# Token sums in four column groups, delta-net logits from one operand, two recurrences at a time, and a changed plan

## The chip, the core and the metric

The kernel runs on one core of one Trainium2 chip. The metric is the device time of one execution in microseconds (us). Its engines are TensorE (PE in the profile, its weight loads PEld), VectorE (DVE), ScalarE (ACT), GpSimd (POOL) and SyncE (SP, which only starts DMAs here); each runs its own instructions strictly in order. All weights come from device memory (HBM).

## The reference

A trunk of two layers: a gated delta-net with a SwiGLU network, then a forgetting attention with a SwiGLU network.

```python
# T = 512 tokens, D = 1024; 8 delta-net heads of 128; 16 forgetting-attention heads of 64; D_FF = 2816
def rms_norm(x, w): return x * rsqrt(mean(x * x) + eps) * w

def gated_deltanet_mixer(h, w_in, conv_w, a_log, dt_bias, out_norm, w_out):
    q, k, v, z, b_logit, a_in = split(h @ w_in)              # b_logit, a_in: 8 + 8 columns
    q, k, v = silu(causal_depthwise_conv(q, k, v; conv_w))   # 4 taps
    q, k = l2_normalize(q) * 128 ** -0.5, l2_normalize(k)    # per token and head
    beta, g = sigmoid(b_logit), -exp(a_log) * softplus(a_in + dt_bias)
    # per head: S_t = a_t (I - b_t k_t k_t^T) S_{t-1} + b_t k_t v_t^T,  o_t = S_t^T q_t
    o = gated_delta_rule_chunked(q, k, v, g, beta)           # triangular solve in chunks, state S carried on
    return (rms_norm(o, out_norm) * silu(z)) @ w_out

for layer in range(2):
    h = rms_norm(x, pre_mix_norm[layer])
    mix = gated_deltanet_mixer(h) if layer == 0 else forgetting_attention(h, shared k, v, gates of x)
    x = x + rms_norm(mix, post_mix_norm[layer])
    f = (silu(gate) * up) @ w_ffn_out                        # gate, up = rms_norm(x) @ w_ffn_in
    x = x + rms_norm(f, post_ffn_norm[layer])
```

## The kernel before

**Layout.** Activations lie with features on the 128 partitions and the 512 tokens along the free dimension, eight tiles for D = 1024. Weights come in units of 512 KB, eight 128x128 blocks each. Values are split into a high and a low half in a 32-bit matmul format (`fp32r`): ACT rounds the high half (`wh` of a weight, the first part of a `b` or `h` pair of an activation), DVE or POOL subtracts it to get the low half (`wl`, the second part). `product` then makes three matmuls of 512 columns per block: high by high, low by high, high by low. A unit is 24 matmuls into one PSUM bank. There are three banks for these projections (`prj`), two for general use (`mid`), two small ones (`sm`) and one for outputs (`ob`).

**The start.** `main` loads the gains, eight x tiles (`a`), the first weights and the constants, splits x times gain into eight b pairs, and sums the squares of x into one tile (`w_124`) on ACT and DVE. The first unit of keys, k0, goes block by block beside `w_small`, 16 columns with the logits of beta and the decay; per block the logits take three matmuls of their own, of 16 columns. The sums of squares are reduced over features by `token_sums`: for each chunk of 128 tokens a matmul whose weights are the 128x128 squares and whose moving operand is one column of ones; it is in plain fp32, which PE runs as two passes. DVE and POOL turn the result into `tokr` and `tokn`, four PE transposes spread `tokn`, ACT copies the rows as n0.rs, and the task `gates` makes beta and the decays. The constants negb, identb and SLR are cast on DVE.

**The delta-net part.** Units follow in the order k0 to k7 (with z0 to z2 between), z3 to z7, then q0, v0, q1, v1 and so on to v7. Behind each unit a task works on: `k_post`, `q_post` (both use `token_sums` for the norms), `v_post`, `z_post`. `inverse` inverts the chunks' 32x32 triangular blocks on DVE for all heads at once; `merge` puts a pair of heads' blocks together into 128x128, by 32x32 and 64x64 matmuls (into `mid`). `recurrence(hd)` then walks four chunks in series: state times keys on PE (`sm<-S,b`), rhs on DVE, a matmul (`sm<-rhs,b`), y on ACT, a matmul to the new state (`sm<-y,w`), S on DVE; the outputs go through `ob`. At the end the output o is scaled, transposed and gated, and split into the b pair `og[hd]`. A recurrence starts when the inverse, q and v of its head are there and the recurrence of the head before is done (signal `s{hd-1}`).

**What sets the order.** Nothing is issued as it is written. A planner (`Plan`) notes each instruction with a cost, tasks are generators that are resumed when what they wait for is done by these costs, and `ordered` then groups the instructions, sorts them in four rounds of list scheduling by the same costs, and issues them; what it gives is each engine's fixed order. Tiles come from rings ("b" has 23, "w" and "a" 8), and a ring's tiles are first written in the order in which they were asked for: an output tile of a later head's convolution is not written before the og pair that was asked for ahead of it. `next_halves` decides by the planned backlog of DVE (over 4 us) whether POOL makes a unit's low half. All instructions are recorded in one line of `Item.issue`, L102 of the profile, so the tile names tell the place.

Of the kernel before, what the change touches and what calls it, by code (L numbers as in the profile page):

```python
# [17 lines left out]
P = 128  # L18
T = 512
# [101 lines left out]
class Plan:  # L121
# [80 lines left out]
    def cost(self, eng, op, out, ins, kw):  # L202

        n = 1
        for d in out.shape[1:]:
            n *= d
        psum = any("PSUM" in str(a.space) for a in ins)
        if eng == "SP" or op == "dma_start":
            return n * 4 * out.shape[0] / 380e3, 2.0
        if eng == "PE":  # L210
            w = ins[0]
            rows, cols = w.shape[0], out.shape[0]
            if w.dtype == F32R:
                t = max(0.109, n / 2400 + 0.0135)
            elif w.dtype == BF16:
                t = n / 2400 + 0.01
            elif op == "transpose":
                t = 0.109
            elif rows <= 32:
                t = 0.026  # L220
            elif rows <= 64:
                t = 0.117
            elif cols == 64:
                t = 0.112 * n / P
            else:
                t = 2 * max(0.111, n / 1200)
            self.grid = (w.dtype == F32R, rows <= 32, rows <= 64, cols <= 64)
            return t, 0.2
        if eng == "ACT":
            m = 1  # L230
            for d in ins[0].shape[1:]:
                m *= d
            t = (m + (172 if psum else 224)) / 1200
            if not isinstance(kw.get("scale", 1.0), float):
                t += 0.09
            if kw.get("accum_out") is not None:
                t += 0.19
            return t, 0.06
        if eng == "POOL":
            if op == "memset":  # L240
                return 0.1 + n / 960, 0.06
            return (0.5 + n * 0.13 if kw.get("op") == ALU.pow else 0.1 + n * 2.28e-3), 0.06
        if op == "tensor_reduce":
            n = 1
            for d in ins[0].shape[1:]:
                n *= d
        if op == "transpose":
            return n * 2.05e-3, 0.06
        fast = op in ("tensor_copy", "tensor_scalar", "memset") and not psum
        t = (n / (2 if fast else 1) + (207 if op == "scalar_tensor_tensor" else 155)) / 960  # L250
        if op == "tensor_scalar" and n > 32:
            t += 0.055
        return t, 0.06
# [179 lines left out]
def trunk(  # L433
# [221 lines left out]
    def next_halves():  # L655

        i = len(ready)
        landing()
        late = plan.free["DVE"] - plan.now()
        slow = late > 4.0 and used[0] < i  # L660
        for go in halve(dve=POOL if slow else DVE):
            go()
        landing()
        signal(f"half{i}")
# [60 lines left out]
            dve.tensor_tensor(out=acc[:, tok], in0=acc[:, tok], in1=sq[:, tok], op=ALU.add)  # L725

    def token_sums(ps, src, chunks):
        for c in chunks:
            PE.matmul(ps[:, c : c + 1], lhsT=src[:, ck(c)], rhs=ones[:, 0:1], start=True, stop=True)

    def token_rsqrt(acc, tok, r, use):

# [210 lines left out]
    def gates(ps, n0):  # L943
        yield ("n0.rs0",)
        ba = small([P, NC, 16], "ba", 1)
        yield from token_logits(ps, n0, ba, 1)
        ealog = small([P, GH], "ealog", 1)
        ACT.activation(ealog, heads_sb[:, 0:8], AF.Exp)
        ta = small([P, NC, GH], "sp", 5)
# [227 lines left out]

    def recurrence(hd):
        kT, AT, E = KA[hd // 2][0][:, hd % 2], KA[hd // 2][1][:, hd % 2], EG[hd // 2][:, hd % 2]
        yield (f"T{hd // 2}", f"q{hd}", f"v{hd}") + ((f"s{hd - 1}",) if hd else ()) + ("#mid",)  # L1180
        qT, PT = Q[hd]
        vu = V[hd]
        ps = mid()
# [3 lines left out]
        for c in range(NC - 1):  # L1187
            DVE.tensor_scalar(
                out=kd[:, ck(c)], in0=ps[:, ck(c)], scalar1=E[:, c * P + P - 1 : c * P + P], scalar2=None, op0=ALU.mult
            )  # L1190
        ms = small([P, NC], "ms", 2)
        junk = small([P, P], "junk", 1)
        o = w_tile()
        S = None
        for c in range(NC):
            rhs = vu[:, ck(c)]
            if S is not None:
                yield (plan.ready(S), "#sm", "#ob")
                ps = sm()
                PE.matmul(ps[:, :P], lhsT=kT[:, ck(c)], rhs=S, start=True, stop=True)  # L1200
                rhs = small([P, P], "rhs", 2)
                DVE.scalar_tensor_tensor(
                    out=rhs, in0=ps[:, :P], scalar=eGn[:, c, hd : hd + 1], in1=vu[:, ck(c)], op0=ALU.mult, op1=ALU.add
                )
# [3 lines left out]
            yield (plan.ready(rhs), "#sm")  # L1208
            ps = sm()
            PE.matmul(ps[:, :P], lhsT=AT[:, ck(c)], rhs=rhs, start=True, stop=True)  # L1210
            y = small([P, P], "y", 2)
            ACT.activation(y, ps[:, :P], AF.Copy, scale=w_t[:, c, hd : hd + 1])
            yield (plan.ready(y), "#sm", "#ob")
            if c < NC - 1:
                ps = sm()
                PE.matmul(ps[:, :P], lhsT=kd[:, ck(c)], rhs=y, start=True, stop=True)
                S2 = small([P, P], "S", 3)
                if S is None:
                    DVE.tensor_copy(S2, ps[:, :P])
                else:  # L1220
                    DVE.scalar_tensor_tensor(
                        out=S2, in0=S, scalar=egl[:, c, hd : hd + 1], in1=ps[:, :P], op0=ALU.mult, op1=ALU.add
                    )
# [324 lines left out]
    for kind, hd in GDN_ORDER:  # L1548
        add(w_gdn["qkvz".index(kind) * GH + hd], DVE)
        if (kind, hd) == ("k", 0):  # L1550
            add(w_small[0], DVE, cols=16)
    out_units(w_gdn_out, 0, KT, eng)

    def ffn_units(layer):
# [24 lines left out]
    def main():  # L1579
# [69 lines left out]
        for kind, hd in GDN_ORDER:  # L1649
# [7 lines left out]
            if (kind, hd) == ("k", 0):  # L1657
                yield ("#prj",)
                ws, pb = [unit(), unit()], prj()
                for k in range(KT):  # L1660
                    product(ps, ws[0], k, h[k], k == 0, k == KT - 1)
                    product(pb[:16], ws[1], k, h[k], k == 0, k == KT - 1)
                    yield (plan.ready(h[min(k + 1, KT - 1)][:, 1]),)
                spawn(gates(pb, n0), -3)
            else:
# [136 lines left out]
```

## Time and profile before

| | us |
|---|---|
| median of 3 runs | 1345.64 (1343.53 to 1346.58) |
| the profiled execution | 1346.76 |
| its span, first to last instruction | 1345.0 |
| PE busy | 1324.7 |
| DVE busy | 770.7 |
| ACT busy | 588.7 |
| POOL busy | 121.3 |

The span is what the profile's rows add up to; the execution's own time has a little around it. Busy shares are means over stages with different limits, so the parts below are read stage by stage: windows give the busy time and TensorE's granted clock (1.00 is 2.4 GHz, 0.50 is 1.2 GHz) in a stretch, the timeline gives single instructions with the idle time ahead of them and what ended it.

### The profile page before, as it was taken

The page shows a single profiled execution, that of the slowest core. Times are in us where ns is not written, and L with a number is a line of the kernel's source. Part 1 is how long each engine was busy: PE and PEld are TensorE (multiplying, and loading weights), DVE is VectorE, ACT ScalarE, POOL GpSimd, SP SyncE. Part 2 cuts the span into 40 slices and gives each one's busy share as a digit, 9 for nine tenths or more (in the row PEclk, how much of TensorE's full clock was granted, in tenths as well). Part 3 has the DMA queues.
Part 4 walks back from the last instruction along what each step waited for, and adds up shares of the span by engine and source line. Part 5 has one row for each costly group of instructions (what it writes and reads, how often), then busy time and mean ns, then how long its engine had stood idle before and what let it go on. Part 6 is the DMA issues. An engine that isn't in the chain of part 4 may idle for free.

```text
span 1345.0 us, 18447 instructions
## 1 busy us (share of the span) xinstructions
PE 1324.7 (98%) x7290; PEld 1105.5 (82%) x7290; DVE 770.7 (57%) x1352; ACT 588.7 (44%) x1111; POOL 121.3 (9%) x109
## 2 busy tenths in 40 slices
PE   8999998999999999999999999999999999999998
PEld 5788887888988888888889787777998888888886
DVE  6978876665864442234448577687675444442223
ACT  5474455555542222232236365685653322233221
POOL 1021000001410000000003321200220000000000
PEclk8999997999999999999999999999999999999999
DMA  6312220113233323332341322210423333333221
GB/s 200 97 47 95 79 64 32 48 48 122 83 110 94 95 89 98 97 107 94 96 139 34 95 82 64 63 49 1 126 79 94 94 94 99 103 97 96 77 95 63
DMA packets 36390, 115.65 MB, mean 86 GB/s; under 512 B 6304, under 2 KB 6560, under 8 KB 36304
## 3 DMA queue, kind: packets, MB, share of 16 engines
q1 hardware_dynamic: 34432, 111.95, 26.5%
q10 hardware_dynamic: 1872, 2.53, 0.6%
q8 instruction: 57, 0.93, 0.3%
q14 instruction: 29, 0.24, 0.1%
HBM read 112.30 MB, written 2.16 MB: 85 GB/s over the span
## 4 chain that ended last, share of the span: by engine, by line
PE 96%; DVE 1%; ACT 1%; DMA 1%; issue 1%; POOL 0%; DVEq 0%; POOLq 0%; ACTq 0%
PE prj L102 76%; PE mid L102 8%; PE sm L102 7%; PE ob L102 6%; DVE b L102 0%; DVE w L102 0%; DMA gains_sb<-in_gains_dram 0%; DMA conv_sb<-in_conv_dram 0%; ACT w L102 0%; ACT b L102 0%; ACT wh L102 0%; DVE h L102 0%; DVE wl L102 0%; DVE a L102 0%; POOL fo L102 0%
## 5 line engine op out<-in xcount | busy, mean ns | idle before, releaser
L102 PE MATMUL prj<-h,wh 128*128 128x512 f32 x1760 | 567.2, 395 | 0.0
L102 ACT ACTIVATE wh<-wf 128x1024 fp32r<-128x1024 f32 (+3 forms) x200 | 207.6, 1039 | 453.6 <-PE prj L102 211.0
L102 PEld LDWEIGHTS prj<-h,wh 128*128 128x128 f32 x1760 | 331.3, 188 | 66.2
L102 PE MATMUL prj<-h,wl 128*128 128x512 f32 x880 | 343.4, 390 | 0.0
L102 DVE TENSOR_TENSOR wl<-wf,wh 128x1024 fp32r<-128x1024 f32 (+2 forms) x182 | 222.8, 1224 | 167.5 <-ACT wh L102 166.4
L102 PE MATMUL prj<-b,wh 128*128 128x512 f32 (+2 forms) x1024 | 303.2, 371 | 3.5 <-DVE b L102 2.8
L102 PEld LDWEIGHTS prj<-b,wh 128*128 128x128 f32 (+1 forms) x1024 | 181.8, 187 | 38.1 <-DVE b L102 4.2
L102 PEld LDWEIGHTS prj<-h,wl 128*128 128x128 f32 x880 | 165.9, 189 | 30.9
L102 PE MATMUL prj<-b,wl 128*128 128x512 f32 (+1 forms) x504 | 182.7, 362 | 0.4 <-DVE wl L102 0.4
L102 DVE TENSOR_TENSOR w<-prj,w 128x512 f32<-128x512 f32 (+1 forms) x90 | 62.2, 691 | 205.9 <-PE prj L102 200.5
L102 PEld LDWEIGHTS prj<-b,wl 128*128 128x128 f32 x504 | 95.0, 188 | 13.7 <-DVE wl L102 1.2
L102 PE MATMUL prj<-wh,b 128*128 128x512 f32 x260 | 88.2, 399 | 0.0
L102 DVE TENSOR_TENSOR w<-w,w 128x512 f32<-128x512 f32 (+1 forms) x123 | 74.9, 620 | 15.6 <-ACT w L102 11.5
L102 ACT ACTIVATE b<-w 64x512 fp32r<-64x512 f32 (+1 forms) x92 | 56.8, 628 | 17.0 <-DVE w L102 16.4
L102 POOL TENSOR_TENSOR wl<-wf,wh 128x1024 fp32r<-128x1024 f32 x17 | 42.9, 2525 | 206.2 <-ACT wh L102 194.0
L102 PEld LDWEIGHTS prj<-wh,b 128*128 128x128 f32 x260 | 49.0, 188 | 10.1 <-issue 0.7
L102 PE MATMUL prj<-wl,b 128*128 128x512 f32 x130 | 50.6, 390 | 0.0
L102 DVE TENSOR_TENSOR b<-w,b 128x512 fp32r<-128x512 f32 (+1 forms) x60 | 46.4, 775 | 0.9 <-ACT b L102 0.5
L102 ACT ACTIVATE b<-sm,m 128x256 f32<-128x256 f32 (+3 forms) x64 | 33.4, 524 | 23.7 <-DVE m L102 23.4
L102 PE MATMUL prj<-h,b 128*128 128x256 f32 x288 | 42.7, 284 | 0.0
L102 DVE TENSOR_REDUCE m<-sm 128x1 f32<-128x256 f32 (+3 forms) x64 | 30.6, 486 | 15.5 <-PE sm L102 15.1
L102 PEld LDWEIGHTS prj<-h,b 128*128 128x128 f32 x288 | 38.0, 192 | 0.0
(215 smaller groups left out, 1531.4 us busy)
## 6 DMA issues: line engine op xcount, KB each, us to landing
wf<-in_w_ffn_in_dram SPq DMA_DIRECT2D x88, 512.0 KB
wf<-in_w_gdn_dram SPq DMA_DIRECT2D x31, 512.0 KB
wf<-in_w_down_dram SPq DMA_DIRECT2D x22, 512.0 KB
wf<-in_w_ffn_out_dram SPq DMA_DIRECT2D x16, 512.0 KB
wf<-in_w_gdn_out_dram SPq DMA_DIRECT2D x8, 512.0 KB
wf<-in_w_q_dram SPq DMA_DIRECT2D x8, 512.0 KB
wf<-in_w_k_dram SPq DMA_DIRECT2D x8, 512.0 KB
wf<-in_w_v_dram SPq DMA_DIRECT2D x8, 512.0 KB
```

Of the source, the lines that this page charges most:

```text
L102: self.call(*[real(v) for v in self.args], **{k: real(v) for k, v in self.kw.items()})
```

## The change

Four things are changed. `token_sums` makes four matmuls per chunk, each with 32 tokens of the chunk as weights, into partitions 0 to 31, 32 to 63 and so on of the result, that is, into four groups of 32 columns of the PE array. The delta-net's logits are made as the attention's gate logits already are: both weight halves lie side by side in one operand of 32 columns, so a block takes two matmuls instead of three (`thin_product`), and `token_logits` adds the two halves after the transposes. `recurrence` waits for the head before the last instead of the last (`s{hd-2}`), with more buffers for its small tiles. The planner takes 5 us instead of 2 for a DMA on ACT's queue to land, 0.03 us for a 32-column matmul in fp32, and gives no low half to POOL before n0.rs is signalled.

```diff
--- before.py
+++ after.py
@@ -206,7 +206,7 @@
             n *= d
         psum = any("PSUM" in str(a.space) for a in ins)
         if eng == "SP" or op == "dma_start":
-            return n * 4 * out.shape[0] / 380e3, 2.0
+            return n * 4 * out.shape[0] / 380e3, 2.0 if eng == "SP" else 5.0
         if eng == "PE":
             w = ins[0]
             rows, cols = w.shape[0], out.shape[0]
@@ -222,6 +222,8 @@
                 t = 0.117
             elif cols == 64:
                 t = 0.112 * n / P
+            elif cols == 32:
+                t = 0.03
             else:
                 t = 2 * max(0.111, n / 1200)
             self.grid = (w.dtype == F32R, rows <= 32, rows <= 64, cols <= 64)
@@ -657,7 +659,7 @@
         i = len(ready)
         landing()
         late = plan.free["DVE"] - plan.now()
-        slow = late > 4.0 and used[0] < i
+        slow = late > 4.0 and used[0] < i and "n0.rs0" in signals
         for go in halve(dve=POOL if slow else DVE):
             go()
         landing()
@@ -725,8 +727,11 @@
             dve.tensor_tensor(out=acc[:, tok], in0=acc[:, tok], in1=sq[:, tok], op=ALU.add)
 
     def token_sums(ps, src, chunks):
+
         for c in chunks:
-            PE.matmul(ps[:, c : c + 1], lhsT=src[:, ck(c)], rhs=ones[:, 0:1], start=True, stop=True)
+            for b in range(4):
+                PE.matmul(ps[ck(b, 32), c : c + 1], lhsT=src[:, c * P + b * 32 : c * P + b * 32 + 32],
+                          rhs=ones[:, 0:1], start=True, stop=True)
 
     def token_rsqrt(acc, tok, r, use):
 
@@ -943,7 +948,7 @@
     def gates(ps, n0):
         yield ("n0.rs0",)
         ba = small([P, NC, 16], "ba", 1)
-        yield from token_logits(ps, n0, ba, 1)
+        yield from token_logits(ps, n0, ba)
         ealog = small([P, GH], "ealog", 1)
         ACT.activation(ealog, heads_sb[:, 0:8], AF.Exp)
         ta = small([P, NC, GH], "sp", 5)
@@ -1177,7 +1182,7 @@
 
     def recurrence(hd):
         kT, AT, E = KA[hd // 2][0][:, hd % 2], KA[hd // 2][1][:, hd % 2], EG[hd // 2][:, hd % 2]
-        yield (f"T{hd // 2}", f"q{hd}", f"v{hd}") + ((f"s{hd - 1}",) if hd else ()) + ("#mid",)
+        yield (f"T{hd // 2}", f"q{hd}", f"v{hd}") + ((f"s{hd - 2}",) if hd > 1 else ()) + ("#mid",)
         qT, PT = Q[hd]
         vu = V[hd]
         ps = mid()
@@ -1188,8 +1193,8 @@
             DVE.tensor_scalar(
                 out=kd[:, ck(c)], in0=ps[:, ck(c)], scalar1=E[:, c * P + P - 1 : c * P + P], scalar2=None, op0=ALU.mult
             )
-        ms = small([P, NC], "ms", 2)
-        junk = small([P, P], "junk", 1)
+        ms = small([P, NC], "ms", 3)
+        junk = small([P, P], "junk", 2)
         o = w_tile()
         S = None
         for c in range(NC):
@@ -1198,7 +1203,7 @@
                 yield (plan.ready(S), "#sm", "#ob")
                 ps = sm()
                 PE.matmul(ps[:, :P], lhsT=kT[:, ck(c)], rhs=S, start=True, stop=True)
-                rhs = small([P, P], "rhs", 2)
+                rhs = small([P, P], "rhs", 3)
                 DVE.scalar_tensor_tensor(
                     out=rhs, in0=ps[:, :P], scalar=eGn[:, c, hd : hd + 1], in1=vu[:, ck(c)], op0=ALU.mult, op1=ALU.add
                 )
@@ -1208,13 +1213,13 @@
             yield (plan.ready(rhs), "#sm")
             ps = sm()
             PE.matmul(ps[:, :P], lhsT=AT[:, ck(c)], rhs=rhs, start=True, stop=True)
-            y = small([P, P], "y", 2)
+            y = small([P, P], "y", 3)
             ACT.activation(y, ps[:, :P], AF.Copy, scale=w_t[:, c, hd : hd + 1])
             yield (plan.ready(y), "#sm", "#ob")
             if c < NC - 1:
                 ps = sm()
                 PE.matmul(ps[:, :P], lhsT=kd[:, ck(c)], rhs=y, start=True, stop=True)
-                S2 = small([P, P], "S", 3)
+                S2 = small([P, P], "S", 5)
                 if S is None:
                     DVE.tensor_copy(S2, ps[:, :P])
                 else:
@@ -1548,7 +1553,7 @@
     for kind, hd in GDN_ORDER:
         add(w_gdn["qkvz".index(kind) * GH + hd], DVE)
         if (kind, hd) == ("k", 0):
-            add(w_small[0], DVE, cols=16)
+            add(w_small[0], DVE, cols=16, thin=True)
     out_units(w_gdn_out, 0, KT, eng)
 
     def ffn_units(layer):
@@ -1659,7 +1664,7 @@
                 ws, pb = [unit(), unit()], prj()
                 for k in range(KT):
                     product(ps, ws[0], k, h[k], k == 0, k == KT - 1)
-                    product(pb[:16], ws[1], k, h[k], k == 0, k == KT - 1)
+                    thin_product(pb, ws[1], k, h[k])
                     yield (plan.ready(h[min(k + 1, KT - 1)][:, 1]),)
                 spawn(gates(pb, n0), -3)
             else:
```

Two places show what moves in the engines' orders.

DVE at the program's start, before (`b` are the split activations, `wl` weights' low halves, `w_124` the sum of squares, `w_115` the constants' tile):

```order
L102 SCALAR_TENSOR_TENSOR b_113<-a_87,gains_sb,b_113 128x512
L102 TENSOR_TENSOR wl_128<-wf_99,wh_119 128x512
L102 CAST negb<-w_115 128x128
L102 TENSOR_TENSOR w_124<-w_124,w_130 128x512
L102 SCALAR_TENSOR_TENSOR b_138<-a_104,gains_sb,b_138 128x512
L102 TENSOR_TENSOR w_124<-w_124,w_144 128x512
L102 SCALAR_TENSOR_TENSOR b_149<-a_109,gains_sb,b_149 128x512
L102 TENSOR_TENSOR w_124<-w_124,w_157 128x512
```

and after, where the tile of constants is called `w_126`:

```order
L102 TENSOR_TENSOR wl_116<-wf_87,wh_112 128x512 x2
L102 TENSOR_TENSOR w_124<-w_124,w_128 128x512
L102 SCALAR_TENSOR_TENSOR b_132<-a_103,gains_sb,b_132 128x512
L102 SCALAR_TENSOR_TENSOR b_137<-a_108,gains_sb,b_137 128x512
L102 SCALAR_TENSOR_TENSOR b_142<-a_114,gains_sb,b_142 128x512
L102 TENSOR_TENSOR w_124<-w_124,w_151 128x512
L102 TENSOR_TENSOR wh_159<-wf_119,wh_159 128x8x16
L102 TENSOR_TENSOR w_124<-w_124,w_162 128x512
L102 SCALAR_TENSOR_TENSOR b_169<-a_121,gains_sb,b_169 128x512
```

The first b tile and the cast of negb are gone from here, and the two parts of the first low half are next to each other. In the order after, negb stands here, behind the last sum of squares and `tokr`:

```order
L102 TENSOR_TENSOR w_124<-w_124,w_232 128x512
L102 TENSOR_TENSOR wl_256<-wf_172,wh_238 128x1024
L102 CAST identb<-cst_sb 128x128
L102 TENSOR_SCALAR tokr_284<-sm_258 128x4
L102 CAST negb<-w_126 128x128
L102 CAST SLR<-w_126 128x128
```

The cast has moved behind 19 rows of sums, b tiles and low halves.

PE at the end of the unit v4 (`prj_1997`) before; `b_455`, `b_844` and `b_1500` belong to one recurrence, `cst_sb` rows are transposes, and `mid_2194` begins the merge of the second pair of heads, whose rows go on until the next unit, `prj_2277`, begins 19 rows further on:

```order
L102 MATMUL prj_1997<-h_565,wh_1548 128x512
L102 MATMUL sm_2138<-y_2134,w_2034 128x128
L102 MATMUL ob_2140<-y_2134,b_1500 128x128
L102 MATMUL sm_2147<-S_2142,b_455 128x128
L102 MATMUL sm_2149<-ones,a_2105 128x1 x3
L102 MATMUL ob_2156<-S_2142,b_1500 128x128
L102 MATMUL sm_2149<-ones,a_2105 128x1
L102 MATMUL sm_2163<-rhs_2158,b_844 128x128
L102 MATMUL ob_2170<-y_2167,b_1500 128x128
L102 MATMUL mid_2187<-cst_sb,w_2072 128x128 x4
L102 MATMUL mid_2194<-a_2097,b_939 32x32 x16
```

and after, behind the last product of q4 (`prj_1897`); `w_1883` and `w_1901` belong to the recurrences of heads 0 and 1:

```order
L102 MATMUL prj_1897<-h_531,wh_1586 128x512
L102 MATMUL sm_1982<-rhs_1976,b_777 128x128
L102 MATMUL sm_1986<-S_1951,b_352 128x128
L102 MATMUL ob_1988<-S_1951,b_1476 128x128
L102 MATMUL sm_1997<-rhs_1990,b_777 128x128
L102 MATMUL sm_1999<-y_1992,w_1883 128x128
L102 MATMUL ob_2003<-y_1992,b_1379 128x128
L102 MATMUL sm_2010<-S_2005,b_352 128x128
L102 MATMUL ob_2013<-S_2005,b_1379 128x128
L102 MATMUL sm_2018<-rhs_2015,b_777 128x128
L102 MATMUL sm_2020<-y_2001,w_1901 128x128
L102 MATMUL ob_2024<-y_2001,b_1476 128x128
```

The rows of two recurrences now alternate, and they stand one unit earlier, behind q4. From the first of them to the first product of v4 (`prj_2186`) there are 44 rows without a projection, with the end of head 1's recurrence and the merge of the second pair among them.

## Rows read from the trace of the kernel before

**Rows 1.** The page, first part: busy us, share and instructions of each engine.

```profile
PE 1324.7 (98%) x7290; PEld 1105.5 (82%) x7290; DVE 770.7 (57%) x1352; ACT 588.7 (44%) x1111; POOL 121.3 (9%) x109
```

**Rows 2.** Waits of PE: waiting for whom: us in total, times, longest.

```profile
PE mid L102 <- DVE w L102: 4.5, 4, 3.0
PE prj L102 <- DVE b L102: 2.8, 2, 2.6
```

**Rows 3.** Stretches: length, busy us by engine (PE, PEld, DVE, ACT, POOL), clock, DMA, GB/s.

```profile
6.00:12.00 6.00, 2.73 (x8) 1.27 (x8) 3.35 (x7) 6.00 (x13) 0.00 (x0) 0.99 1.01 313
12.00:20.00 8.00, 6.94 (x23) 3.02 (x22) 8.00 (x11) 5.34 (x9) 2.86 (x1) 0.79 0.74 262
20.00:30.00 10.00, 9.55 (x43) 6.33 (x43) 4.75 (x10) 2.19 (x3) 2.20 (x1) 0.83 0.34 107
...
30.00:214.00 184.00, 184.00 (x1154) 154.57 (x1152) 151.62 (x321) 101.22 (x215) 17.06 (x14) 1.00 0.24 75
214.00:234.00 20.00, 14.12 (x148) 11.89 (x147) 13.74 (x29) 9.67 (x23) 1.01 (x1) 0.57 0.08 27
```

**Rows 4.** Timeline of 0 to 30 us: start, us, engine, operation, [idle before, releaser].

```profile
6.23 0.49 PE L102 MATMUL prj<-b,wh 128*128 128x512 f32 x1 [0.55 <-ACT wh L102]
...
9.69 0.23 DVE L102 CAST negb<-w 128x128 bf16<-128x128 f32 x1 [2.65 <-DMA w<-in_cst_dram]
...
11.23 0.73 PE L102 MATMUL prj<-b,wh 128*128 128x512 f32 x2 [2.61 <-DVE b L102]
...
16.24 3.55 DVE L102 SCALAR_TENSOR_TENSOR b<-a,gains_sb,b 128x512 fp32r<-128x512 f32 x2
16.38 2.86 POOL L102 TENSOR_TENSOR wl<-wf,wh 128x1024 fp32r<-128x1024 f32 x1 [15.94 <-ACT wh L102]
...
20.45 1.05 PE L102 MATMUL sm<-ones,w 128*128 128x1 f32 x8 [1.34 <-DVE w L102]
...
26.02 0.39 PE L102 MATMUL prj<-b,wl 128*128 128x512 f32 x1
26.25 0.62 PE L102 MATMUL prj<-b,wh 128*128 128x512 f32 x2
...
27.18 0.60 PE L102 MATMUL mid<-cst_sb,tokn 128*128 128x128 f32 x4
...
27.81 0.60 ACT L102 ACTIVATE w<-mid 128x512 f32<-128x512 f32 x1 [10.47 <-PE mid L102]
```

**Rows 5.** Timeline of PE, 213 to 230 us.

```profile
213.43 0.49 PE L102 MATMUL sm<-y,w 128*128 128x128 f32 x2
...
216.74 0.80 PE L102 MATMUL ob<-y,b 128*128 128x128 f32 x2 [0.56 <-ACT y L102]
220.52 1.09 PE L102 MATMUL mid<-cst_sb,w 128*128 128x128 f32 x4 [2.98 <-DVE w L102]
221.54 1.06 PE L102 MATMUL mid<-a,b 32*32 32x32 f32 x32
...
229.89 0.79 PE L102 MATMUL prj<-h,wh 128*128 128x512 f32 x1
```

**Rows 6.** Timeline of PE at a set of four token sums.

```profile
81.34 0.95 PE L102 MATMUL sm<-ones,a 128*128 128x1 f32 x8
82.15 0.58 PE L102 MATMUL mid<-b 128*128 128x128 f32 x3
```

**Rows 7.** PE at a merge's third step; weight loads by form (count, busy us, mean ns).

```profile
198.13 0.22 PE L102 MATMUL mid<-b,w 32*32 32x32 f32 x2
...
198.64 0.19 PE L102 MATMUL mid<-w,b 32*32 32x32 f32 x1
198.76 0.49 PE L102 MATMUL sm<-rhs,b 128*128 128x128 f32 x2
...
L102 PEld LDWEIGHTS mid<-b,w 32*32 32x32 f32 x128 | 2.8, 118 | 1.8 <-DVE w L102 0.9 <-issue 0.7
L102 PEld LDWEIGHTS prj<-b,wh 128*32 128x32 f32 x16 | 1.7, 109 | 1.9
```

## The prediction

> **What bounds the kernel now.** I read the page's busy shares first: the TensorE (PE) is busy for 98% of the span [rows 1]. So time is only to be had in three ways: PE's idle time, PE's half clock, and PE's own instructions. The waits of PE say who lets it idle: VectorE (DVE) above all, with one wait of 3.0 us and one of 2.6 us [rows 2]. The table of stretches says where: between 6 and 30 us, and between 214 and 234 us. From 30 to 214 us PE is never idle and its granted clock is 1.00 [rows 3].
>
> The start has two losses. PE is idle for 3.27 us of 6 to 12, 1.06 us of 12 to 20 and 0.45 us of 20 to 30; and the mean granted clock is 0.79 and 0.83 in the two later stretches, which is 1.2 GHz for about 3.4 us of each, some 1.7 us lost in each [rows 3]. The timeline shows the cause. DVE casts negb from a constant, waited 2.65 us for that constant's DMA, and the sums and b tiles queued behind the cast came late: PE waited 2.61 us for a b tile at 11.23. Later two b tiles took DVE 3.55 us while POOL made a wl half for 2.86 us beside it, and PE's first token sums waited 1.34 us until 20.45 [rows 4].
>
> The second hole, 214 to 234 us, has 14.12 us of work in 20 us at a clock of 0.57 [rows 3]: 5.9 us idle; and a mean of 0.57 is about 2.8 us at 2.4 GHz and 17.2 us at 1.2 GHz, in which some 11.2 us of work would have taken half: 5.6 us. Together 11.5 us. The timeline shows PE with nothing but the end of one recurrence, the transposes of its output (2.98 us wait) and the merge of a later pair of heads [rows 5].
>
> **The start: constants later, logits in one operand.** In the new order DVE's cast is behind the token statistics, and PE's first product waits for two weight halves ahead of the b tile on ScalarE (ACT), where b came first before. From durations of 0.6 to 0.75 us for a half, a square or a b tile I walk ACT's new order: b0 is ready at about 7.3, so PE starts 1.1 us later than its 6.23 [rows 4], but b1 to b7 then follow without the 2.65 us wait; the last is there at about 16.7, and DVE's last sum of squares at about 19.6. Up to 27.5 us, where the token transposes are done [rows 4] and the rest of the unit k1 begins, PE of before has (27.5 - 6.23) - 4.5 idle = 16.8 us of work, of which 3.4 are lost to half clock: 13.4 us at full clock. The logits take 8 matmuls less (16 instead of 24, 512 columns each); one is 0.23 us by the starts 26.02 and 26.25 [rows 4], so 1.8 us. That leaves 11.6 us, and I leave one dip of the clock in (1.7 us): 7.3 + 11.6 + 1.7 = 20.6 us, say 20.8, for what stood at 27.5. **Gain 6.7 us.** Bounds: 4 if one more wait of 2.6 us appears, 8.5 if the dip goes too. DVE's additional 128x64 addition of the two logit halves is hidden, since PE has the products of k1 meanwhile; uncovered it is 0.2 to 0.3 us. Taking the wl halves from POOL at the start puts two splits of 1.2 us on DVE; what covers them is that DVE's 2.65 us wait is gone.
>
> **The token sums.** 92 chunks are summed, 17 sets of four and 12 of two. Now a chunk is one matmul in two passes with a 128-column weight load each; a set of four takes 81.34 to 82.15 = 0.81 us, 0.101 us a pass [rows 6]; by that, all 184 passes take 18.6 us. The change makes them 736 passes of 32 columns. No row has such a pass. The nearest are the 32x32 passes of the merge: 48 from 198.13 to 198.64, 10.6 ns each, and 0.12 us from the last to the next kind's start [rows 7]. In two of that step's three matmuls the rows of the array are the same and the column groups differ, as here; these two alone are 32 passes in the 0.51 us, 15.9 ns each. The far bound is the 109 ns that a weight load of 128x32 shows [rows 7]. I take 13 ns, since the passes of one streamed column are nearest to the merge's, and 0.2 us for the switch in and out of each of 29 sets: 736 x 0.013 + 29 x 0.2 = 15.4 us. **Gain 3.2 us** (5.0 at 10.6 ns, 1.1 at 15.9 ns, a loss of 67 at 109 ns). A set of four gains, a set of two gains about nothing. All of it lies on PE's path.
>
> **Two recurrences at a time.** A recurrence is a chain of PE, DVE, PE, ACT, PE; three of its links took 213.43 to 216.74, 1.1 us each [rows 5]. Waiting for the head before the last lets PE put a second chain into these gaps, so the 11.5 us hole at 214 to 234 should go. But the new order makes a hole of its own, earlier: between the last product of q4 (prj_1897) and the first of v4 (prj_2186) stand 44 rows without a projection, because v4's bank waits for a convolution whose output tile waits for head 0's gated output. In these rows head 1 has 8 links in a row, 8.8 us, and then the merge of the second pair, which took 221.54 to 229.89, 8.35 us, at half clock [rows 5]; at full clock and with part of it beside the links I make the stretch 16.6 us, with 9.5 us of PE work in it. So 7 us idle and, with only its later part at half clock, 3 us more: **cost 10 us.** Bounds: 3 (the chains and the merge fill each other's gaps) and 14. Net of the old hole 1.5 us are gained, between 8.5 gained and 2.5 lost. The further buffers of ms, junk, rhs, y and S cost only space.
>
> **The rest.** The longer latency that the planner now assumes on ACT's queue only moves DMA issues of constants; after the delta-net part the two orders are nearly the same but for the sums.
>
> **The sum.** The profiled span is 1345.0 us, its execution took 1346.76, and the median of the runs, 1345.64, is 0.64 above the span. 1345.0 - 6.7 - 3.2 - 1.5 = 1333.6 us of span, 1334.2 on the scale of the median; I say **1334.5 us**.
>
> **Rivals.** *First, the start's gain is given back.* DVE is busy for 151.62 of 184 us between 30 and 214 [rows 3], so its inverse may come only 3.7 us earlier (the token scale that ended ACT's 10.47 us wait and was done at 28.4 [rows 4] comes at about 24.7), while PE arrives at the first merge 8.5 us earlier. PE then waits up to 4.8 us there, with up to 1.7 us of half clock: 1339 to 1341 us. Against it: PE has not waited once in these 184 us, so there is some slack.
>
> *Second, the two chains fill the gaps* and the new hole costs 3 us: 1327.5 us. For it: in the old hole the merge and the chain lay one behind the other; against it: the links are serial.
>
> *Third, the passes of the sums don't overlap their loads.* A pass with 128 columns took 0.101 us [rows 6], so 32 columns at that rate take 25 ns: 736 x 0.025 + 5.8 = 24.2 us, a loss of 5.6 in place of a gain of 3.2: 1343.3 us. From 28 ns a pass the kernel is slower than before ((18.6 - 5.8 + 8.2) / 736, where 8.2 is the gain of start and holes), and at 109 ns it is at 1405 us. Against it: 10.6 ns in the merge, whose loads show 118 ns each [rows 7] and so must overlap. The Trainium skill, TensorE: Matmul & The Clock Gate, Part 3 (The mechanism), says that a weight load overlaps matmuls in flight only where the row group differs, and the four column groups here share all rows; its section on LDWEIGHTS gives columns / 1.2 ns, 27 ns for 32 columns, and by that estimate the sums would lose 7 us. The trace bears it out in part: matmuls of one row group took 15.9 ns a pass, more than 10.6, but less than 27.
>
> *Fourth, the change doesn't run two at a time.* The order shows rows of both heads in turn, so a bank would have to hold the second back; the new hole then has its 14 us: 1338.5 us.
>
> **How the numbers follow.** 2.7 us (0.2%) is about what a measurement of this kernel can tell from no change. The forecast, 1330 to 1338.5 us with the fourth rival as its end, has 0.48; the start given back (to 1342) 0.17; holes filled (1325 to 1330) 0.17; sums at 20 to 30 ns a pass (1343 to 1348) 0.10; sums slower than that 0.08. So faster 0.82, within 0.2% 0.10, slower 0.08. The range, 1326 to 1344, leaves out the last two cases but for the lower edge of the first of them, and the lowest part of the holes filled.
>
> **What would show it.** In the new profile: negb's cast after tokr, and the rest of unit k1 begun at some 21 us instead of 27.5; a set of four sums in 0.55 to 0.65 us from its start to the next kind's; no idle time in 214 to 234, and a stretch with 5 to 8 us idle and a clock near 0.5 between the last q4 product and the first of v4, near 176 to 195 us; all from 240 us on as long as before but for the sums. It would be wrong if PE waited at the first merge, if the sums' passes lay over 25 ns apart, or if the hole before v4 were short.

## The result and the profile after

| | before | after |
|---|---|---|
| median, us | 1345.32 (4 runs) | 1331.12 (1329.01 to 1333.15, 4 runs) |
| ratio, 95% interval | | 0.9897 [0.9884, 0.9909] |
| the profiled execution, us | 1346.76 | 1329.01 |
| its span, us | 1345.0 | 1327.2 |
| PE busy, us | 1324.7 | 1312.5 |

14.2 us less on the medians, where 10.8 to 11.1 were forecast. The profiled execution after is the fastest of its four and that of before is above its median, so the span is 17.8 us shorter; the steps below are compared on these spans. In a second group of runs (r1 below) the changed kernel had 0.9881 [0.9866, 0.9896], so I take 0.9889, the middle of the two, where another kernel is set against it.

Stretches of the changed kernel, columns as in [rows 3]:

```profile
6.00:12.00 6.00, 3.85 (x9) 2.65 (x10) 4.50 (x8) 5.60 (x11) 0.00 (x0) 0.72 1.02 345
12.00:20.00 8.00, 8.00 (x39) 5.06 (x38) 7.78 (x12) 6.89 (x12) 0.00 (x0) 0.99 0.78 287
20.00:30.00 10.00, 10.00 (x79) 8.08 (x79) 8.45 (x19) 4.69 (x8) 1.06 (x1) 1.00 0.57 200
30.00:120.00 90.00, 90.00 (x668) 73.25 (x667) 75.51 (x157) 55.05 (x109) 8.84 (x9) 1.00 0.24 78
...
180.00:200.00 20.00, 16.24 (x178) 13.06 (x176) 12.73 (x36) 11.02 (x35) 2.27 (x3) 0.91 0.08 27
200.00:220.00 20.00, 20.00 (x163) 17.60 (x164) 14.37 (x38) 12.93 (x36) 1.26 (x2) 0.92 0.08 28
220.00:240.00 20.00, 20.00 (x232) 16.65 (x227) 16.12 (x35) 13.22 (x34) 1.01 (x1) 1.00 0.09 28
```

The start has one stretch with a low clock (0.72 in 6 to 12 us) instead of two [rows 3], and no idle time from 12 us on. The old hole at 214 to 234 is gone; a new one stands at 180 to 200, 3.76 us idle, with the clock low on both sides of 200. PE's waits after, to be held against [rows 2]:

```profile
PE prj L102 <- ACT b L102: 2.4, 1, 2.4
PE sm L102 <- DVE S L102: 1.1, 3, 0.6
...
PE mid L102 <- DVE w L102: 1.0, 2, 0.9
```

Where the 17.8 us went can be counted along PE's timeline: the projection matmuls of 512 columns come 24 to a unit, in the same order of units in both kernels. The third unit, k2, begins at 33.70 us before and 26.14 after, and k4 at 44.58 and 37.16, 7.6 and 7.4 us earlier: **7.4 us at the start**. At the 21st unit, where the keys' sums are done, it is 10.1 us: 2.7 more, which are eight sets of sums for the keys. At the 37th unit, in the feed-forward network, it is 17.4: another 7.3 us from the part with queries, values and recurrences, where eight more sets of sums lie. From there to the end 0.4 us are added.

The timeline of the changed kernel at the start, as in [rows 4]:

```profile
8.13 0.50 PE L102 MATMUL prj<-b,wh 128*128 128x512 f32 x1 [2.36 <-ACT b L102]
...
19.97 0.43 PE L102 MATMUL sm<-ones,w 128*32 128x1 f32 x32
20.33 0.50 PE L102 MATMUL prj<-b,wh 128*128 128x512 f32 x1
...
22.51 0.60 PE L102 MATMUL mid<-cst_sb,tokn 128*128 128x128 f32 x4
```

PE starts 1.9 us later than before, for it waits for the b tile behind two weight halves, but from there on it has work all the time, and the transposes come at 22.5 instead of 27.2, with half of the unit k1 already done ahead of them, where before all of k1 stood behind them. The stretch behind q4, the changed kernel's PE timeline:

```profile
185.66 0.46 PE L102 MATMUL sm<-S,b 128*128 128x128 f32 x2 [0.60 <-DVE S L102]
...
187.81 0.46 PE L102 MATMUL sm<-S,b 128*128 128x128 f32 x2 [0.31 <-DVE S L102]
...
195.40 1.11 PE L102 MATMUL mid<-a,b 64*64 64x64 f32 x16 [0.56 <-ACT a L102]
197.40 1.94 PE L102 MATMUL mid<-b,w 64*64 64x64 f32 x16 [0.88 <-DVE w L102]
...
201.32 0.78 PE L102 MATMUL prj<-h,wh 128*128 128x512 f32 x1
```

Many waits of 0.2 to 0.9 us in a row, where the old hole had one of 2.98; the clock falls only near the end of it, so the 64x64 step of the merge takes 1.94 us at half clock. A finer table of the same trace, columns as above:

```profile
196.00:197.00 1.00, 0.52 (x9) 0.38 (x7) 0.90 (x2) 0.04 (x1) 0.83 (x1) 0.71 0.00 0
197.00:203.00 6.00, 5.61 (x30) 4.98 (x31) 3.49 (x10) 3.09 (x6) 0.00 (x0) 0.50 0.01 3
203.00:204.00 1.00, 1.00 (x10) 1.00 (x10) 0.59 (x3) 0.16 (x2) 0.00 (x0) 0.88 0.00 0
```

That is 6.8 us at 1.2 GHz, in which PE is busy for 5.9.

### The profile page after: what moved, and what is told of

Same layout as the page of the kernel before. It is cut to its first block, busy times and chain, and to the rows that moved or that the text cites. A ratio compares the mean times of both kernels' runs of the same rounds, so it can differ in the third digit from the quotient of the medians.

```text
span 1327.2 us, 19520 instructions
## 1 busy us (share of the span) xinstructions
PE 1312.5 (99%) x7834; PEld 1092.3 (82%) x7834; DVE 767.0 (58%) x1354; ACT 590.1 (44%) x1111; POOL 112.4 (8%) x107
## 4 chain that ended last, share of the span: by engine, by line
PE 97%; issue 1%; DVE 1%; ACT 1%; DMA 0%; SPq 0%; DVEq 0%; POOLq 0%; POOL 0%
PE prj L102 77%; PE mid L102 8%; PE sm L102 6%; PE ob L102 6%; DMA a<-in_xT_dram 0%; DVE w L102 0%; ACT wh L102 0%; ACT w L102 0%; DVE h L102 0%; ACT b L102 0%; SPq L102 0%; DVE S L102 0%; ACT h L102 0%; DVE b L102 0%; DVEq L1794 0%
## 5 line engine op out<-in xcount | busy, mean ns | idle before, releaser
L102 PE MATMUL prj<-b,wh 128*128 128x512 f32 (+2 forms) x1008 | 294.6, 368 | 2.4 <-ACT b L102 2.4
L102 PEld LDWEIGHTS prj<-b,wh 128*128 128x128 f32 (+1 forms) x1008 | 179.1, 187 | 33.7 <-ACT b L102 2.5
L102 PE MATMUL prj<-b,wl 128*128 128x512 f32 (+1 forms) x488 | 175.4, 359 | 0.0
L102 DVE TENSOR_TENSOR w<-w,w 128x512 f32<-128x512 f32 (+1 forms) x123 | 79.6, 656 | 21.6 <-ACT w L102 16.9
L102 PEld LDWEIGHTS prj<-wh,b 128*128 128x128 f32 x260 | 48.9, 188 | 10.1 <-issue 0.7
L102 POOL TENSOR_TENSOR wl<-wf,wh 128x1024 fp32r<-128x1024 f32 x15 | 36.6, 2437 | 176.9 <-ACT wh L102 167.8
L102 DVE TENSOR_TENSOR b<-w,b 128x512 fp32r<-128x512 f32 (+1 forms) x60 | 41.9, 703 | 0.9 <-ACT b L102 0.5
```

The lines of the kernel that those rows point to most:

```text
L102: self.call(*[real(v) for v in self.args], **{k: real(v) for k, v in self.kw.items()})
```

## The experiments

Each kernel is the changed one or the one before with the edits shown. What a run is above or below the changed kernel is the difference of the ratios to before, times 1346 us. A ratio has an interval of about 2 us and so such a difference one of about 2.5 us; steps of 1 or 2 us are therefore read from the traces, at the units' starts.

**e1: the sums in 128 columns again, every order kept** (the planner prices one such sum like four of 32 columns).

```diff
+            elif n == 1:
+                t, cols = 0.12, 32
...
-            for b in range(4):
-                PE.matmul(ps[ck(b, 32), c : c + 1], lhsT=src[:, c * P + b * 32 : c * P + b * 32 + 32],
-                          rhs=ones[:, 0:1], start=True, stop=True)
+            PE.matmul(ps[:, c : c + 1], lhsT=src[:, ck(c)], rhs=ones[:, 0:1], start=True, stop=True)
```

> The changed kernel with the token sums as before (one matmul of 128 columns per chunk), planned at the cost of four 32-column ones, so that every engine's order is that of the changed kernel. Theory A (the sums' own PE time): in the two traces the steps from each sum to the next instruction add up to 18.4 us before and 8.9 us after, all on PE's path, so 9.4 us longer than the changed kernel, about 1340.5 us; a set of four takes 0.81 us again. Rival B (my prediction's price of 13 ns a pass and 0.2 us of switches): 3.2 us longer, about 1334.3 us, and the rest of the gain has another source. Rival C (the sums were partly hidden behind waits in the delta-net part): under 2 us.

Measured: 1336.6 us, 0.9926 [0.9911, 0.9941], 5.0 us above the changed kernel. In the trace the third unit begins 1.56 us later (besides the first set of sums, the clock is at 1.2 GHz for 6.8 us at the start instead of 3.4, with the same order), the 37th 7.26 later: 5.7 us from the sixteen sets of four between them. So neither 9.4 nor 3.2; the time alone would not exclude 3.2. Theory A had added up only the steps from sum to sum. The rows show what it left out; e1, then the changed kernel:

```profile
82.68 0.95 PE L102 MATMUL sm<-ones,a 128*128 128x1 f32 x8
83.49 0.49 PE L102 MATMUL prj<-h,wh 128*128 128x512 f32 x1
83.81 0.40 PE L102 MATMUL prj<-h,wl 128*128 128x512 f32 x1
```

```profile
80.58 0.39 PE L102 MATMUL prj<-h,wh 128*128 128x512 f32 x1
80.90 0.43 PE L102 MATMUL sm<-ones,a 128*32 128x1 f32 x32
81.26 0.50 PE L102 MATMUL prj<-h,wh 128*128 128x512 f32 x1
81.60 0.39 PE L102 MATMUL prj<-h,wl 128*128 128x512 f32 x1
```

A set of four takes 0.81 us in e1 (82.68 to 83.49) and 0.36 after (80.90 to 81.26), but the matmul ahead of it takes 0.32 (80.58 to 80.90) where its like takes 0.23: 0.09 us are lost going in. Going out costs both about 0.1, since the matmul behind takes 0.34 (81.26 to 81.60), and 0.32 in e1 (83.49 to 83.81). So a set gains 0.45 - 0.09 - 0.02 = 0.34 us. Two of the sixteen sets lie side by side and take 1.71 us in e1 and 0.64 after; they gain 0.96, the other fourteen 4.8, together the 5.7 us measured. With the first set of the program, ahead of the third unit, it is 6.0 us. A set of two takes 0.36 in e1 and 0.24 after and gains nothing once the ways in and out are paid.

**e2: every 32-column sum made twice** (each planned at half the price).

```diff
-                t = 0.03
+                t = 0.015
...
-            for b in range(4):
+            for b in (0, 1, 2, 3, 0, 1, 2, 3):
```

> The changed kernel with each 32-column sum made twice over the same result, 1472 passes instead of 736, same orders and the same number of switches between kinds. Theory A (a pass costs the 8.5 ns at which the passes of one set start one after the other in the trace of the changed kernel): 736 x 8.5 ns = 6.3 us longer, about 1337.4 us, and a set of four takes 0.63 us instead of 0.36. Rival B (13 ns a pass): 9.6 us longer. Rival C (loads serial, 25 ns a pass): 18 us longer.

Measured: 1335.64 us, 0.9919 [0.9904, 0.9934], 4.0 us above the changed kernel. The trace of e2:

```profile
80.36 0.71 PE L102 MATMUL sm<-ones,a 128*32 128x1 f32 x64
81.00 0.50 PE L102 MATMUL prj<-h,wh 128*128 128x512 f32 x1
```

A set of four takes 0.64 us with 64 passes against 0.36 with 32: 0.28 us for 32 passes, 8.7 ns each. That is theory A; 13 and 25 ns are out. Between the third and the 21st unit lie 256 more passes, and there e2 takes 2.25 us longer, 8.8 ns each. All 736 passes more would be 6.4 us by that, at the upper edge of what the time allows; e2 and the changed kernel also differ in where the clock was low, for e2's stayed at 1.00 through the start.

**e3: DMAs on ACT's queue planned at 2 us again.** PE's order stays the same row for row; on DVE the cast moves ahead, and on ACT the first b tile.

```diff
-            return n * 4 * out.shape[0] / 380e3, 2.0 if eng == "SP" else 5.0
+            return n * 4 * out.shape[0] / 380e3, 2.0
```

> The changed kernel planned with 2 us for DMAs on ACT's queue, as before. PE's order is the same row for row; on DVE the cast of negb stands at its ninth place, ahead of the sums and of most b tiles, and ACT makes the first b tile ahead of the weight halves. Theory A (the cast's wait for the constants' DMA was what the start lost): DVE waits 2 to 3 us there again, PE waits for a b tile behind it by 2 to 3 us and falls to the half clock once more; PE's first product comes 1.9 us earlier, at about 6.2; k1's end is 2 to 4 us later than 26.1 and the time about 1334 us. Rival B (the start's gain is the logits', the sums' and ACT's b tiles'; the cast's wait is hidden): within 1 us of the changed kernel.

Measured: 1333.99 us, 0.9903 [0.9886, 0.992], 1.9 us above the changed kernel. The timeline of e3:

```profile
11.47 0.23 DVE L102 CAST negb<-w 128x128 bf16<-128x128 f32 x1 [2.24 <-DMA w<-in_cst_dram]
...
12.41 4.00 PE L102 MATMUL prj<-b,wh 128*128 128x512 f32 x8 [2.50 <-DVE b L102]
```

The cast waits for its DMA again, a b tile stands behind it, PE waits 2.5 us for that and then works at half clock (6.8 us of it at the start instead of 3.4). The third unit begins at 29.90 instead of 26.14, 3.8 us later: theory A for the mechanism. The interval of the whole time doesn't tell it from rival B.

**e4: one recurrence at a time**, with the old buffers.

```diff
-        yield (f"T{hd // 2}", f"q{hd}", f"v{hd}") + ((f"s{hd - 2}",) if hd > 1 else ()) + ("#mid",)
+        yield (f"T{hd // 2}", f"q{hd}", f"v{hd}") + ((f"s{hd - 1}",) if hd else ()) + ("#mid",)
```

> The changed kernel with the recurrence waiting for the head before it again, and the old numbers of buffers. Theory A (the hole moved and shrank): a hole with about 6 us idle and 5 us lost to the half clock comes back in the last third of the delta-net part while the hole behind q4 stays in part; 5 to 8 us longer than the changed kernel, about 1337 us. Rival B (the new order's gain in the delta-net part comes from the start and the sums alone, the signal only moves the hole): within 2 us.

Measured: 1341.79 us, 0.9963 [0.995, 0.9976], 10.0 us above the changed kernel. PE's waits and two stretches of e4:

```profile
PE mid L102 <- ACT a L102: 4.2, 1, 4.2
PE prj L102 <- ACT b L102: 3.1, 1, 3.1
PE mid L102 <- DVE w L102: 2.9, 3, 2.5
```

```profile
220.00:240.00 20.00, 16.06 (x175) 12.39 (x174) 10.34 (x26) 10.65 (x29) 1.01 (x1) 0.82 0.14 49
240.00:260.00 20.00, 15.76 (x102) 13.39 (x102) 9.25 (x22) 6.68 (x18) 0.00 (x0) 0.75 0.00 1
```

Two holes with 8.2 us idle and half clock. The signal, with its buffers, is needed; B is out, and A's 5 to 8 us lie low.

**r1: the changed kernel again**, on the same chip as r2 to r4.

> The changed kernel once more, unaltered, beside the other kernels of this group and on the same chip. Expected 0.988 to 0.991 of before, about 1331 to 1333 us; its executions should differ by 2 us or more by how often PE falls to the half clock at the start and behind q4.

Measured: 1329.22 us (1329.02 to 1330.16), 0.9881 [0.9866, 0.9896]. The four executions differ by 1.1 us only, less than expected.

**r2: the kernel before with only the recurrence's wait and buffers changed** (the recurrence's lines of the diff).

> The kernel before with only the recurrence's wait (the head before the last) and its buffers changed. Theory A (the old hole is a single recurrence's gaps, and the hole behind q4 comes from how the changed kernel's order happens to place the rows): the hole of 214 to 234 goes, 11.5 us, and a new one costs 3 us or less: 1336 to 1338 us. Rival B (two recurrences at a time always starve v4's bank): a hole of about 5.5 us as in the changed kernel, 1339 to 1340 us. Rival C (the old hole stays): 1344 to 1346 us.

Measured: 1339.8 us, 0.9956 [0.9941, 0.9971], 5.9 us below before. PE's timeline of r2:

```profile
203.18 1.11 PE L102 MATMUL mid<-a,b 64*64 64x64 f32 x16 [0.90 <-ACT a L102]
205.58 1.94 PE L102 MATMUL mid<-b,w 64*64 64x64 f32 x16 [1.29 <-DVE w L102]
```

The old hole goes and a new one comes, 2.2 us idle in the merge with half clock behind it. Rival B is nearest: the signal with its buffers is worth 6 us here, with a hole in its place; the run's start was also slower, its third unit 1.3 us later than before (34.96), with the clock low for longer.

**r3: the kernel before with only the planner's two rules changed.**

> The kernel before with only the planner's two rules changed (5 us for DMAs on ACT's queue, no low half to POOL before n0.rs). Theory A (about half of the start's 7.4 us is the cast's wait, the rest logits, sums and b tiles): the end of k1 is 3.5 to 5 us earlier than 33.7 and the hole of 214 to 234 stays: 1340 to 1342 us. Rival B (all of it is the plan): 6 to 7 us earlier, 1338.5 us. Rival C (the order moves the gain into a longer hole): 1344 us or more.

Measured: 1342.64 us, 0.9976 [0.9966, 0.9986], 3.2 us below before. In the trace the third unit begins at 27.30, 6.4 us earlier than before, rival B's size and not A's; of these 5.2 us are left at the 37th. That does not make the plan nearly all of the start's 7.4 us: r3's clock stayed at 1.00 through the start, while the changed kernel's was low for 3.4 us. The old hole is still there:

```profile
212.80 0.49 PE L102 MATMUL ob<-y,b 128*128 128x128 f32 x2 [0.38 <-ACT y L102]
215.88 1.09 PE L102 MATMUL mid<-cst_sb,w 128*128 128x128 f32 x4 [2.58 <-DVE w L102]
```

**r4: three edits to the changed kernel against its two remaining losses.**

```diff
-            return n * 4 * out.shape[0] / 380e3, 2.0 if eng == "SP" else 5.0
+            return n * 4 * out.shape[0] / 380e3, 5.0 if out.tensor.name.split("_")[0] in ("cst", "w", "heads", "conv") else 2.0
...
+    PQ = {}
...
-        pq = b_pair(F32)
+        pq = PQ[hd]
...
-            if kind in "qv" and hd >= 3:
-                yield (f"s{hd - 3}",)
+            if kind in "qv" and hd >= 4:
+                yield (f"s{hd - 4}",)
+            if kind == "q":
+                yield ("#b",)
+                PQ[hd] = b_pair(F32)
```

> The changed kernel with three edits meant to take away what is left: only the DMAs of constants that aren't needed at once are planned at 5 us, and the gains' at 2 as before, so that the first b tile is made before the second weight half while negb's cast stays late; the b pair of a q unit is asked for before its products, ahead of the next gated output; a q or v unit waits for the recurrence four heads back instead of three. Theory A (both remaining losses are order alone): PE's first product at 6.3 instead of 8.1 us and no wait above 1 us behind it, 1.5 to 2 us gained at the start; the hole behind q4, 3.8 us idle and 1.7 us of half clock, gone or spread, 3 to 5 us gained: 1325 to 1327 us. Rival B (the losses move to the next wait): within 2 us of the changed kernel.

Measured: **1322.81 us, 0.9835 [0.9819, 0.9851]**, the fastest of all, 6.4 us below the changed kernel in the same group. Its page:

```profile
PE 1307.9 (99%) x7834; PEld 1087.3 (82%) x7834; DVE 767.2 (58%) x1353; ACT 588.7 (45%) x1111; POOL 118.0 (9%) x108
```

PE's waits are 1.1 us at most, and the clock is 1.00 from the start to the tail. Rival B is out, and the gain is above theory A's 3 to 5 us for the hole.

**s1: only the first of these edits** (the constants' DMAs late, the gains early). PE's order is the changed kernel's.

> The changed kernel with only the constants' DMAs planned at 5 us and the gains' at 2: the first b tile is made ahead of the weight halves, as before the change, and negb's cast stays late. PE's order is that of the changed kernel row for row. Theory A (PE's late first product costs little, since the tiles behind it come at the rate of ACT and of the x DMAs): PE starts at 6.3 instead of 8.1 us, k1's end is about 0.5 us earlier than 26.1, the time within 1 us of the changed kernel. Rival B (the first wait of 2.4 us is on the path, and the half clock behind it): 2 to 3.5 us faster.

Measured: 1329.57 us, 0.9875 [0.9858, 0.9892]. PE's timeline:

```profile
5.76 0.77 PE L102 MATMUL prj<-b,wh 128*128 128x512 f32 x1
...
9.49 0.52 PE L102 MATMUL prj<-b,wh 128*128 128x512 f32 x1 [1.33 <-ACT b L102]
```

PE begins its first product 2.4 us earlier, at 5.76, waits for a later b tile instead, and the third unit begins at 26.28, within 0.2 us of the changed kernel's. That is theory A: the late first product costs nothing. The time alone doesn't tell it from rival B.

**s2: only the other two edits**, in the delta-net part.

> The changed kernel with only the two edits in the delta-net part of the run before with three edits (a q unit's b pair asked for ahead of its products; units wait for the recurrence four heads back). Theory A (what that run gained is the hole behind q4, 5.5 us, and the start gave 0.5): 0.983 to 0.985 of before, about 1323 to 1325 us, and no half clock between 100 us and the end. Rival B (half of it is the start): 1326 to 1327 us.

Measured: 1323.69 us, 0.9836 [0.9821, 0.9851]. Stretches of s2:

```profile
170.00:190.00 20.00, 20.00 (x176) 17.59 (x176) 15.57 (x41) 11.58 (x32) 2.39 (x1) 1.00 0.25 80
190.00:210.00 20.00, 20.00 (x209) 16.76 (x207) 14.39 (x38) 12.38 (x31) 2.65 (x3) 1.00 0.16 53
```

Theory A: the whole gain of r4 is the hole behind q4. In the trace the third unit begins 0.5 us later than in the changed kernel and the 37th 5.4 earlier: the two edits are worth 5.9 us there. That is net of 2.4 us of waits, 0.1 to 0.6 us each, which s2 has between 262 and 304 us and the changed kernel has not. Which of the two edits did it was not tried.

**s3: POOL may again make low halves before n0.rs.**

```diff
-        slow = late > 4.0 and used[0] < i and "n0.rs0" in signals
+        slow = late > 4.0 and used[0] < i
```

> The changed kernel with POOL again allowed to make low halves before n0.rs. Theory A (POOL beside DVE slows DVE's two-operand work at the start, as in the 3.55 us for two b tiles of the trace before, and the token sums come late): k1's end 1 to 2 us later than 26.1, DVE's b tiles beside POOL's low half take over 1 us again; with the order's changes behind it 1331 to 1336 us. Rival B (the rule is worth nothing, the start's gain is the late cast): k1's end within 0.5 us of the changed kernel.

Measured: 1335.73 us, 0.9925 [0.991, 0.994], 4.8 us above the changed kernel. The timeline of s3 (POOL's row, then DVE's) and PE's longest wait:

```profile
16.37 2.80 POOL L102 TENSOR_TENSOR wl<-wf,wh 128x1024 fp32r<-128x1024 f32 x1 [15.93 <-ACT wh L102]
...
16.90 2.35 DVE L102 CAST identb<-cst_sb 128x128 bf16<-128x128 f32 x1
```

```profile
PE mid L102 <- DVE w L102: 4.7, 4, 3.4
```

The cast of identb takes 2.35 us and ends when POOL's work ends; in the changed kernel, with POOL at rest, it takes 0.22. The third unit begins only 0.7 us later, less than theory A's 1 to 2. The rest, 5.8 us in the trace, is a wait of 3.4 us at 233 us, ahead of the transposes of an output as in the old hole, and the half clock around it, which came with the other order.

**s4: the old logits.**

```diff
-        yield from token_logits(ps, n0, ba)
+        yield from token_logits(ps, n0, ba, 1)
...
-            add(w_small[0], DVE, cols=16, thin=True)
+            add(w_small[0], DVE, cols=16)
...
-                    thin_product(pb, ws[1], k, h[k])
+                    product(pb[:16], ws[1], k, h[k], k == 0, k == KT - 1)
```

> The changed kernel with the delta-net's logits in three matmuls a block of 16 columns again. Theory A (8 matmuls of 0.227 us on PE's path at the start): k1's end 1.8 us later, and whatever the other order does behind q4, 0 to 5 us: 1332 to 1337 us. Rival B (PE waits for b tiles at the start anyway, so the 8 matmuls fill waits): k1's end under 0.7 us later.

Measured: 1339.37 us, 0.9958 [0.9936, 0.998], 9.3 us above the changed kernel. The third unit begins 2.1 us later, theory A's 1.8 for the eight matmuls. Up to the 37th unit it is 10.6 us: 8.6 come from the delta-net part, where PE is idle for 4.5 us more and half clock follows, with a wait of 3.4 us as in s3 among it; that is more than A allowed.

## Why the prediction was right, point by point

**The start**: 6.7 us forecast, 7.4 measured, 0.3 of them the first set of sums. The mechanism is shown by e3: undoing the DMA rule alone, with PE's order kept, brings the cast's wait and 3.8 us back; the b tile that moves with it is worth nothing by s1. s4 shows the eight logit matmuls at 2.1 us, forecast 1.8. That the halves go from POOL to DVE at no cost held too: s3 shows that POOL's work there holds DVE up instead. The 1.1 us for PE's later start was 1.9 and, by s1, is worth nothing by itself. I had left one dip of the clock in, and there is one. The sign that I named for it, the rest of k1 begun at some 21 us, came at 22.86, because half of k1 was already done by then.

**The sums**: 3.2 us forecast, 6.0 measured (e1). The term that was mis-sized is the price of a pass: 13 ns, between the merge's 10.6 and 15.9, where e2 shows 8.7. A set of four took 0.36 us, below the 0.55 to 0.65 that I had named as the sign. The 0.2 us for the switch in and out held (0.09 in, about 0.1 out), only that the old sums paid the way out too. The third rival (25 ns and more) is out. The rule of the Trainium skill that stood beside it, TensorE: Matmul & The Clock Gate, Part 3 (The mechanism), that a weight load overlaps matmuls in flight only where the row group differs, is not borne out here: passes that share all rows and differ in the column group start 8.5 to 8.7 ns apart, each with its own weights.

**Two recurrences**: net 1.5 us forecast (11.5 gone, 10 new). Measured are 7.3 us between the 21st and the 37th unit, less eight sets of sums (3.0 by e1): 4.2 us. The old hole went as forecast, and a new one stands where it was forecast, between the last product of q4 and the first of v4. The mis-sized term is its price: 10 us forecast, 5.9 by s2. The stretch itself was longer than I made it, from 182.5 to 201.3 us; but the second chain's matmuls and the merge filled the gaps of the first to waits of under 1 us, and the clock stayed at 1.00 until 196 and was low for 6.8 us. My 7 us of idle time were 3.8, and that was the error; of the 6.8 us at half clock PE worked 5.9, which cost 3.0, as forecast. By these rows the hole costs 6.7 us. So the second rival was half right. The first rival is out: the stretches from 12 to 180 us have no idle time, and PE never waited at the first merge. The fourth is out by e4.

**The rest** held in the second half: from the 37th unit on only 0.4 us are added. But the prediction's sentence that the longer latency only moves DMA issues of constants is wrong, and against its own account of the start: by e3 the same rule moves DVE's cast and ACT's first b tile, and at the start it is worth 3.8 us.

The terms of the trace are 7.1 (start without its sums), 6.0 and 4.2, together 17.3 of 17.8 us; the last 0.5 are not assigned. The forecast lay low because two terms, a pass of the sums and the idle time of the new hole, were priced too high. The medians, 14.2 us apart, lie about 3 us above the forecast; the two profiled executions lie further apart than they do.

What was not foreseen is how little the parts add up. Undoing one costs 5.0 (sums), 10.0 (recurrences), 4.8 (POOL's rule) and 9.3 us (logits), 29 together, without the 1.9 us of the DMA rule, which are within the interval; all of them together bring 14 to 17. In s3 and s4 the part itself is worth 0.7 and 2.1 us, and most of the rest is a hole like the old one, which the planner's order makes or avoids by small differences at the start. Why its list scheduling falls on one or the other was not tried, and neither were the planner's 0.03 us for a 32-column sum or the added buffers by themselves.

## What to carry to other kernels

Price a set of tiny matmuls as passes times the step between their starts, plus what the neighbours lose going in and out; four column groups pay for sets of 32 passes and bring nothing for sets of 16. Where an engine runs strictly in order, put work that waits for a DMA behind everything that others wait for, and give the planner the landing time that the trace shows (here 4.75 us from issue at 4.94 to the cast at 9.69). When a list scheduler sets the order, measure a part inside the whole and look where the holes went: one part's undoing brought a hole of 3.4 us elsewhere (s3, s4), and s2's two edits to what v4's bank waits for (a tile asked for ahead, and a wait one head further back) were worth 5.9 us, about as much as all the new sums.

## What was not expected of the hardware

A 32-column fp32 pass over 128 rows, with its own weights and one streamed column, starts 8.7 ns after the last in another column group (e2). A DVE cast that takes 0.22 us alone took 2.35 us beside a POOL instruction of 2.80 us and ended with it (s3), as two b tiles took 3.55 us in [rows 4]. The Trainium skill, SBUF — State Buffer, Who interferes with whom, says that the two engines share a port pair which one of them holds for a whole instruction, and the trace agrees. The clock fell to 1.2 GHz after one idle stretch of 2.4 us at the start, and in s1 after one of 1.33 us, but in e2 one of 1.85 us at the same place left it at 2.4 GHz, as did a row of waits of 0.2 to 0.6 us from 183 to 192 us in the changed kernel; so the length of one idle stretch doesn't decide it alone, and what does is not shown here. In r4, with PE's waits at 1.1 us or less, it never fell before the tail.
